# Block products of a triangular inverse with four blocks per matmul, zero-padded low-rank corrections, and another order of the parts

## The chip, the core and the metric

The kernel runs on one core of one Trainium2 chip. The core has five engines that run their own instruction queues and wait for each other by semaphores: TensorE (PE, matmuls into PSUM), VectorE (DVE), ScalarE (ACT), GpSimd (POOL) and SyncE (SP, which here issues nearly all DMAs). The metric is the device time of one execution in microseconds (us). The time before is 2999.29 us, the median of three runs (2991.41 to 3010.68).

## What is computed

Two layers of a hybrid network over 256 context tokens and 256 latent tokens, 1024 channels. Each layer has three token mixers (RWKV-7 in both directions, RG-LRU, neighbourhood attention), gates that merge them, and a gated MLP. The change touches the first mixer. Its core per head and direction is

```python
def step(S, inp):
    r_t, w_t, k_t, v_t, kk_t, a_t = inp
    sa = jnp.einsum('bhvk,bhk->bhv', S, -kk_t)
    S = (S * w_t[:, :, None, :] + sa[..., None] * (kk_t * a_t)[:, :, None, :]
         + v_t[..., None] * k_t[:, :, None, :])
    return S, jnp.einsum('bhvk,bhk->bhv', S, r_t)
```

with decay and a-gate made from low-rank products:

```python
w_log = -jax.nn.softplus(-(p['rwkv_w0'][d] + w_lo @ p['rwkv_w_up'][d])) - 0.5
a = jax.nn.sigmoid(p['rwkv_a0'][d] + a_lo @ p['rwkv_a_up'][d])
```

The kernel does the recurrence in chunks of 64 tokens. For each chunk it needs the inverse of a 64x64 unit triangular matrix: 2 heads, 2 directions and 8 chunks make 32 such matrices per pair of heads.

## The kernel before

All weights of a matmul come as one 512 KB tile from HBM. They are split into a high part (`wh`, ScalarE, L226) and a low part (`wl`, VectorE or GpSimd, L229), and `mm3` (L247 to L249) issues three matmuls of fp32r type per 128 rows. Activations have the same two parts (`hh`, `hl`). Tokens are 512 columns in layer 0. In layer 1 only 256 columns are wanted for most outputs. These `pj`, `pbr`, `wo`, `fg`, `fu`, `fo` matmuls are the bulk of the work.

A layer's mixers run over 8 pairs of heads. Per pair, the parts are letters in `CFG[l]['order']`: `1` and `2` make keys and prepare the next pair (`rw_key`, `rw_prep`), `g` the masked Gram products (`Gm`), `v` transposes (`bt`, and `BK` scaled in place), `i` the triangular solve of the 32x32 diagonal blocks on VectorE (`rw_inv`, L636 to L664), `I` the two products that fill the off-diagonal block (`rw_inv2`), `T` the sequence over 8 chunks (`rw_seq`: matmuls `r`, `sa`, `sp`, `yp`), `o`, `O`, `B` the output. The other letters are the other mixers: `X`, `Y`, `a`, `b`, `S` RG-LRU, `Q`, `A`, `P` attention, and `G`, `N` gate projections. `pri` gives a letter a priority. A scheduler turns order and priorities into one instruction list per engine, which the engine then follows strictly.

In `rw_inv2` VectorE transposes the solved blocks three times: L674 makes `T1` (tile `AT`), which the first product needs, L675 and L676 make parts of `TT` (tile `RT`). L676 is needed by the second product. The first product (L681, `Q<-AT,Gm`) is 32 matmuls of 32x32 by 32x32 in fp32, the second (L687, `Q<-RT,AT`) as many; the profile records each fp32 matmul as two, each with its own weight load. ScalarE copies each PSUM bank of 16 results back with one instruction (L682, L688). After them a DMA (L691) puts `KR` over the lower half of `Gm`, which `r` (L723) reads.

In `rw_prep` each direction multiplies the low-rank weights by activations that hold a high part in one half of the 128 rows and a low part in the other: `lh` (both halves the high weight) by all rows, then `ll` (low weights) by the 64 rows of the high part only:

```python
nc.tensor.matmul(pw, lhsT=lh[:, dc], rhs=self.wS, start=True, stop=False)
nc.tensor.matmul(pw, lhsT=ll[0:64, dc], rhs=self.wS[0:64], start=False, stop=True)
```

(L511, L512; L518, L519 for `pa`.) That is 2 such pairs for each of 2 directions, 8 pairs of heads and 2 layers.

## Time and profile before

| | before |
|---|---|
| median of three runs | 2999.29 us |
| profiled execution | 2999.59 us |
| span of its instructions | 2997.8 us |
| TensorE busy | 2834.2 us (95%) |
| VectorE busy | 1964.5 us (66%) |
| ScalarE busy | 1512.0 us (50%) |
| GpSimd busy | 595.7 us (20%) |
| mean granted TensorE clock | 0.957 |

The profile's page gives busy time per engine. Its views of waits, lines, stretches and the timeline say what an engine waited for and how long an instruction took. Matmuls overlap, so a matmul's own duration is longer than the distance between the starts of two. The distance is what it costs. Engine lines with one-line groups give busy time as the union of overlapping instructions.

### The profile page before, as it was taken

What the parts mean: (1) busy time and instruction counts of PE and PEld (TensorE: products, weight loads), DVE (VectorE), ACT (ScalarE), POOL (GpSimd) and SP (SyncE); (2) the same over time, 40 slices, a digit from 0 to 9 for tenths busy, and PEclk for the clock granted to TensorE, in tenths of its full rate; (3) what the DMA queues carried; (4) which work ended last, traced back from release to release, by engine and by line L of the source; (5) the groups of instructions that cost most, each with busy time, mean ns of one, the idle gap of its engine ahead of it and who ended that gap; (6) DMA issues with size and microseconds to landing.
All of it is one profiled execution on the core that took longest, in us unless ns stands there. A gap on an engine that the chain in (4) does not pass through costs nothing. (4 is left out here: it accounts for less than half of the span.)

```text
span 2997.8 us, 51813 instructions
## 1 busy us (share of the span) xinstructions
PE 2834.2 (95%) x20144; PEld 2263.7 (76%) x20144; DVE 1964.5 (66%) x3947; ACT 1512.0 (50%) x2917; POOL 595.7 (20%) x618
## 2 busy tenths in 40 slices
PE   7999999999999999989999998999999999989998
PEld 5777777777767677787778887777777777678898
DVE  6768777677776744475443268687778768755774
ACT  3565554556546542353333356655655665634453
POOL 2121120211202212200002211222221221212440
PEclk9999999999999999999999999999999998979899
DMA  6322122221222345755653452222222222236663
GB/s 226 94 70 74 56 89 64 72 68 53 87 69 68 106 158 182 255 184 182 218 175 92 121 172 83 65 78 77 67 72 82 64 64 78 87 104 211 219 195 115
DMA packets 159222, 344.30 MB, mean 115 GB/s; under 512 B 47488, under 2 KB 74368, under 8 KB 158976
## 3 DMA queue, kind: packets, MB, share of 16 engines
q1 hardware_dynamic: 152064, 334.69, 34.8%
q10 hardware_dynamic: 6912, 6.29, 0.7%
q8 instruction: 159, 2.61, 0.4%
q14 instruction: 87, 0.71, 0.1%
HBM read 301.08 MB, written 25.17 MB: 109 GB/s over the span
## 5 line engine op out<-in xcount | busy, mean ns | idle before, releaser
L226 ACT ACTIVATE wh<-wr 128x1024 fp32r<-128x1024 f32 (+1 forms) x402 | 420.1, 1046 | 537.4 <-PE pj L248 195.1
L247 PE MATMUL pj<-hh,wh 128*128 128x512 f32 (+1 forms) x1440 | 561.4, 391 | 22.6 <-DVE k L432 14.7
L229 DVE TENSOR_TENSOR wl<-wr,wh 128x1024 fp32r<-128x1024 f32 (+1 forms) x320 | 411.2, 1285 | 250.8 <-ACT wh L226 240.4
L249 PE MATMUL pj<-hh,wl 128*128 128x512 f32 (+1 forms) x1440 | 551.7, 384 | 8.2 <-POOL wl L229 4.1
L248 PE MATMUL pj<-hl,wh 128*128 128x512 f32 (+1 forms) x1440 | 551.3, 383 | 0.0
L247 PEld LDWEIGHTS pj<-hh,wh 128*128 128x128 f32 x1440 | 282.7, 196 | 83.0 <-issue 24.9
L249 PEld LDWEIGHTS pj<-hh,wl 128*128 128x128 f32 x1440 | 282.7, 197 | 61.8 <-issue 8.8
L229 POOL TENSOR_TENSOR wl<-wr,wh 128x1024 fp32r<-128x1024 f32 (+1 forms) x82 | 199.0, 2429 | 629.9 <-ACT wh L226 602.7
L248 PEld LDWEIGHTS pj<-hl,wh 128*128 128x128 f32 x1440 | 283.2, 197 | 47.1 <-issue 8.9
L741 POOL TENSOR_TENSOR sg<-SV,gC 64x128 f32<-64x128 f32 x192 | 114.3, 595 | 337.3 <-DVE SV L756 272.6
L660 DVE TENSOR_TENSOR itmp<-AT 128x126 f32<-128x126 f32 (+22 forms) x496 | 140.0, 282 | 11.2
L662 DVE TENSOR_TENSOR AT<-AT,itmp 128x126 f32<-128x126 f32 (+22 forms) x496 | 134.7, 272 | 10.8
L586 PEld LDWEIGHTS gram<-KR,BK 64*128 64x128 f32 x1024 | 120.5, 196 | 26.3 <-issue 13.9
L586 PE MATMUL gram<-KR,BK 64*128 64x128 f32 (+1 forms) x1024 | 136.6, 290 | 0.9 <-DVE Gm L589 0.4
L247 PE MATMUL fo<-fh,wh 128*128 128x256 f32 (+1 forms) x418 | 130.3, 312 | 0.0
L249 PE MATMUL fo<-fh,wl 128*128 128x256 f32 (+1 forms) x418 | 130.2, 311 | 0.0
L248 PE MATMUL fo<-fl,wh 128*128 128x256 f32 (+1 forms) x418 | 129.8, 310 | 0.0
L247 PE MATMUL fg<-hh,wh 128*128 128x256 f32 (+1 forms) x384 | 128.2, 336 | 1.1 <-ACT hh L403 1.1
L247 PE MATMUL fu<-hh,wh 128*128 128x256 f32 (+1 forms) x384 | 125.3, 327 | 2.7 <-DVE fgs L1356 2.0
L248 PE MATMUL fg<-hl,wh 128*128 128x256 f32 (+1 forms) x384 | 126.8, 331 | 0.0
L249 PE MATMUL fg<-hh,wl 128*128 128x256 f32 (+1 forms) x384 | 126.5, 330 | 0.0
L249 PE MATMUL fu<-hh,wl 128*128 128x256 f32 (+1 forms) x384 | 125.5, 328 | 1.0 <-DVE wl L229 1.0
(337 smaller groups left out, 6321.0 us busy)
## 6 DMA issues: line engine op xcount, KB each, us to landing
wr<-in_w_in SPq DMA_DIRECT2D x180, 512.0 KB, 3.3
aw<-in_ada_w SPq DMA_DIRECT2D x96, 512.0 KB, 4.6
wr<-in_ffn_w_in SPq DMA_DIRECT2D x96, 512.0 KB, 4.1
wr<-in_w_branch SPq DMA_DIRECT2D x48, 512.0 KB, 3.6
wr<-in_ffn_w_out SPq DMA_DIRECT2D x36, 512.0 KB, 3.6
wr<-in_w_out SPq DMA_DIRECT2D x24, 512.0 KB, 4.7
Gm<-KR SPq DMA_DIRECT2D x32, 256.0 KB, 4.3
wr<-in_ffn_w_out SPq DMA_DIRECT2D x18, 384.0 KB, 3.1
```

The lines of the kernel that those rows point to most:

```text
L226: nc.scalar.activation(hi, raw, AF.Copy)
L229: eng.tensor_tensor(lo, raw, hi.bitcast(F32), op=ALU.subtract)
L247: nc.tensor.matmul(o, lhsT=a, rhs=xh[k][:, n0:n1], start=(first and k == 0), stop=False)
L248: nc.tensor.matmul(o, lhsT=a, rhs=xl[k][:, n0:n1], start=False, stop=False)
L249: m = nc.tensor.matmul(o, lhsT=b, rhs=xh[k][:, n0:n1], start=False, stop=(last and k == kt - 1))
L586: nc.tensor.matmul(ps[:, i, 0:nx], lhsT=BK[hs, d, c, :], rhs=KR[hs, 0:nx, d, c, :], start=True, stop=True)
L660: eng.tensor_tensor(tmp, Ap[:, q + 1:32, q:q + 1].to_broadcast([P, nt, ns]), Tf[:, q:q + 1, 0:2 * ns:2].to_broadcast([P, nt, ns]), op=ALU. ...
L662: eng.tensor_tensor(Tf[:, q + 1:32, 0:2 * ns:2], Tf[:, q + 1:32, 0:2 * ns:2], tmp, op=ALU.subtract)
L741: nc.gpsimd.tensor_tensor(sg[64 * h:64 * h + 64], SV[0:64, i, :, h], gC[:, :, h, i:i + 1].to_broadcast([64, 2, 64]), op=ALU.mult)
```

## The change

1. The first product takes four blocks at once: the weights are four blocks side by side (32 rows, 128 columns), and the moving operand is four blocks of `T1` (128 columns). The result is 128x128, of which only the four 32x32 diagonal blocks are wanted. 8 matmuls replace 32. The second product is changed in the same way. ScalarE copies the diagonal blocks out with four instructions per bank in place of one.
2. With `f1` at 3 the blocks that the first product reads (`A10`) are first copied by VectorE into a corner of `BK` (32 rows, 1024 elements), and the `KR` to `Gm` DMA is issued in `rw_inv`, behind that copy, and no longer behind the products.
3. `ll` holds zeros where it was not read, and its matmuls use all 128 rows. VectorE makes two 64x256 pieces in place of one of 128x512, and GpSimd clears two 64x256 pieces.
4. Other orders, priorities and choices of engine in `CFG` for both layers; in layer 0 `oy` goes from 1 to 0, which makes the output transposes and gate product in one piece of 512 columns.

```diff
-  'order': '||g|ovOiXQIa||YbGSTA|12NPB|',
-  'oy': 1,
+  'order': '||g||o|vXQO|ia|I|Yb|GAT12SBNP||',
+  'oy': 0,
...
-  'order': 'gvGiIXabYSQA12TNPoOB',
+  'order': 'gGXviYaIb|SQA12TNPoOB',
...
-        self.split(lw[:, :512], lh, ll)
+
+        nc.scalar.activation(lh, lw[:, :512], AF.Copy)
+        for x in range(2):
+            rs, cs = slice(64 * x, 64 * x + 64), slice(256 * x, 256 * x + 256)
+            nc.vector.tensor_tensor(ll[rs, cs], lw[rs, cs], lh[rs, cs].bitcast(F32), op=ALU.subtract)
+            nc.gpsimd.memset(ll[rs, 256 - 256 * x:512 - 256 * x].bitcast(F32), 0.0)
...
-            nc.tensor.matmul(pw, lhsT=ll[0:64, dc], rhs=self.wS[0:64], start=False, stop=True)
+            nc.tensor.matmul(pw, lhsT=ll[:, dc], rhs=self.wS, start=False, stop=True)
...
-            nc.tensor.matmul(pa, lhsT=ll[64:128, dc], rhs=self.aS[64:128], start=False, stop=True)
+            nc.tensor.matmul(pa, lhsT=ll[:, dc], rhs=self.aS, start=False, stop=True)
...
-            ps = self.ps("q", "Q").rearrange("p (j t) -> p j t", t=32)
-            for i in range(16):
-                j = 16 * g + i
-                nc.tensor.matmul(ps[96:128, i, :], lhsT=A10[:, j], rhs=T1[0:32, j, :], start=True, stop=True)
-            nc.scalar.activation(T1[96:128, 16 * g:16 * g + 16, :], ps[96:128], AF.Copy, scale=-1.0)
+
+            ps = self.ps("q", "Q").rearrange("p (m a t) -> p m a t", a=4, t=32)
+            for m in range(4):
+                j = slice(16 * g + 4 * m, 16 * g + 4 * m + 4)
+                nc.tensor.matmul(ps[:, m].rearrange("p a t -> p (a t)"), lhsT=A10[:, j],
+                                 rhs=T1[0:32, j, :].rearrange("p a t -> p (a t)"), start=True, stop=True)
+            for a in range(4):
+                nc.scalar.activation(T1[96:128, 16 * g + a:16 * g + 16:4, :], ps[32 * a:32 * a + 32, :, a], AF.Copy, scale=-1.0)
```

The copied block is made by code that was there (`f1`):

```python
A10 = u["BK"][0:32, 0].rearrange("p c (x t) -> p (c x) t", t=32)
...
nc.vector.tensor_copy(A10, A0[0:32, :, 32:64])
for h in range(2):
    nc.sync.dma_start(G[0:64, 0, :, :, h], u["KR"][64 * h:64 * h + 64, 0])
```

TensorE's list at the inverse of the fourth pair of layer 1 (`pj` projections, `Q` the inverse products, `pa` low-rank products, `kst` the key norms, `r` the first step of the sequence). Before:

```order
L247 MATMUL pj_21745<-hh_15607,wh 128x512
L681 MATMUL Q<-AT,Gm 32x32 x32
L248 MATMUL pj_21745<-hl_15615,wh 128x512
L249 MATMUL pj_21745<-hh_15607,wl 128x512
L518 MATMUL pa<-aS,lh 128x512
L519 MATMUL pa<-aS,ll 128x512
L247 MATMUL pj_21745<-hh_15608,wh 128x512
L248 MATMUL pj_21745<-hl_15616,wh 128x512
L249 MATMUL pj_21745<-hh_15608,wl 128x512
L687 MATMUL Q_20598<-RT,AT 32x32 x16
L687 MATMUL Q_20616<-RT,AT 32x32 x16
L247 MATMUL pj_21745<-hh_15609,wh 128x512
```

and of the change:

```order
L249 MATMUL pj_20511<-hh_15231,wh 128x512
L689 MATMUL Q<-AT,BK 128x128 x8
L250 MATMUL pj_20511<-hl_15239,wh 128x512
L251 MATMUL pj_20511<-hh_15231,wl 128x512
L697 MATMUL Q_20289<-RT,AT 128x128 x4
L697 MATMUL Q_20298<-RT,AT 128x128 x4
L490 MATMUL kst<-cst,ta 128x2 x4
L250 MATMUL pj_20404<-hl_15234,wh 128x512
```

Two matmuls of 512 columns stand between the products where seven stood, and the next pair's keys and low-rank products come after the products, no longer ahead of them.

TensorE's list ahead of the inverse of the last pair of layer 1 (`pt`, `ao` attention; `pbr` the merge, `sa` the second step of the sequence). Before:

```order
L1063 MATMUL pt<-cst,pr 128x128 x4
L1074 MATMUL ao<-PT,vt 64x256
L1063 MATMUL pt<-cst,pr 128x128 x2
L1074 MATMUL ao<-PT,vt 64x256 x3
L1080 MATMUL ao<-PT,vt 64x64 x8
L681 MATMUL Q<-AT,Gm 32x32 x32
L687 MATMUL Q_25026<-RT,AT 32x32 x16
L687 MATMUL Q_25044<-RT,AT 32x32 x16
L723 MATMUL r_25310<-SV,Gm 128x128 x2
```

and of the change:

```order
L250 MATMUL pj_24947<-hl_15239,wh 128x256
L251 MATMUL pj_24947<-hh_15231,wl 128x256
L251 MATMUL pj_24704<-hh_15227,wl 128x512
L689 MATMUL Q<-AT,BK 128x128 x8
L249 MATMUL pj_24704<-hh_15228,wh 128x512
L250 MATMUL pj_24704<-hl_15236,wh 128x512
L697 MATMUL Q_24589<-RT,AT 128x128 x4
L251 MATMUL pj_24704<-hh_15228,wl 128x512
L249 MATMUL pj_24704<-hh_15229,wh 128x512
L250 MATMUL pj_24704<-hl_15237,wh 128x512
```

Projections now stand right up to the products. Between the last `bt` and the first `Q` of this pair the list of before has 9 matmuls of 512 columns and 46 of 256 among `pj` and `pbr`; the changed one has 37 and 72.

VectorE's list at the start of the solve of the fourth pair of layer 1 (`AT<-Gm` the transposes, `BK<-Gm` the new copy, `itmp` the first step of the solve, `xb` and `s` work of other mixers). Before:

```order
L636 STREAM_TRANSPOSE AT<-Gm 32x1024 x2
L984 TENSOR_TENSOR k<-sw 128x256
L649 COPY AT<-AT 64x1024
L660 TENSOR_TENSOR itmp<-AT 128x31
L662 TENSOR_TENSOR AT<-AT,itmp 128x31
```

and of the change:

```order
L643 STREAM_TRANSPOSE AT<-Gm 32x1024 x2
L231 TENSOR_TENSOR wl<-wr,wh 128x1024
L653 COPY BK<-Gm 32x1024
L656 COPY AT<-AT 64x1024
L842 SCALAR_TENSOR_TENSOR xb<-pj_20017,pv_13329,xb 128x2x254
L667 TENSOR_TENSOR itmp<-AT 128x31
```

The copy stands ahead of the solve and is one more instruction in that chain.

## Rows read from the trace of the kernel before

**Rows 1.** The page, part 1: busy us, share of span, instructions.
```profile
PE 2834.2 (95%) x20144; PEld 2263.7 (76%) x20144; DVE 1964.5 (66%) x3947; ACT 1512.0 (50%) x2917; POOL 595.7 (20%) x618
```

**Rows 2.** Cores: span, mean granted TensorE clock.
```profile
core 0: 2997.8 us, clock 0.957
```

**Rows 3.** TensorE's waits: us in total, times, longest us.
```profile
PE Q L681 <- DVE AT L674: 18.1, 12, 4.8
```

**Rows 4.** Timeline of TensorE at a low-rank pair: start us, us, instruction.
```profile
73.51 0.39 PE L247 MATMUL pj<-hh,wh 128*128 128x512 f32 x1
73.74 0.39 PE L248 MATMUL pj<-hl,wh 128*128 128x512 f32 x1
...
74.19 0.39 PE L511 MATMUL pw<-wS,lh 128*128 128x512 f32 x1
74.51 0.50 PE L512 MATMUL pw<-wS,ll 64*128 64x512 f32 x1
74.94 0.50 PE L247 MATMUL pj<-hh,wh 128*128 128x512 f32 x1
```

**Rows 5.** TensorE by line and form: count, busy us, mean ns, idle before.
```profile
L586 PE MATMUL gram<-KR,BK 64*128 64x128 f32 x768 | 110.7, 293 | 0.7 <-DVE Gm L589 0.4
...
L687 PE MATMUL Q<-RT,AT 32*32 32x32 f32 x1024 | 42.8, 205 | 0.8 <-DVE RT L676 0.8
...
L681 PE MATMUL Q<-AT,Gm 32*32 32x32 f32 x1024 | 39.8, 200 | 18.1 <-DVE AT L674 18.1
...
L519 PE MATMUL pa<-aS,ll 64*128 64x512 f32 x32 | 16.4, 514 | 0.0
L512 PE MATMUL pw<-wS,ll 64*128 64x512 f32 x32 | 16.3, 509 | 0.0
```

**Rows 6.** Timeline of TensorE: eight recorded fp32 128x128 passes in a row.
```profile
108.76 1.03 PE L621 MATMUL bt<-cst,BK 128*128 128x128 f32 x8
```

**Rows 7.** The page, part 5: weight loads of 64x128 in fp32.
```profile
L586 PEld LDWEIGHTS gram<-KR,BK 64*128 64x128 f32 x1024 | 120.5, 196 | 26.3 <-issue 13.9
```

**Rows 8.** Stretches around layer 1's last pair: us, busy by engine, PEclk, DMA, GB/s.
```profile
2480.00:2595.00 115.00, 107.44 (x760) 83.07 (x759) 83.53 (x184) 63.72 (x132) 22.95 (x31) 0.92 0.22 69
2595.00:2660.00 65.00, 50.14 (x379) 39.45 (x380) 45.35 (x119) 28.41 (x67) 5.06 (x5) 0.71 0.32 96
```

**Rows 9.** Stretches of 3.4 us: second products of one pair, then what follows.
```profile
524.40:527.80 3.40, 3.40 (x69) 2.70 (x68) 0.00 (x0) 0.88 (x2) 0.21 (x1) 1.00 0.47 113
527.80:531.20 3.40, 3.40 (x10) 2.63 (x9) 0.00 (x0) 0.60 (x2) 0.60 (x3) 0.50 0.02 5
```

**Rows 10.** The eleven half-clock stretches right behind inverse products: first, last, sum.
```profile
268.40:275.20 6.80, 6.80 (x56) 4.24 (x52) 4.37 (x3) 3.52 (x5) 0.00 (x0) 0.50 0.20 41
...
2528.00:2538.20 10.20, 10.20 (x81) 8.22 (x81) 4.79 (x8) 5.54 (x11) 1.99 (x4) 0.50 0.40 103
sum 78.20, PE 77.73 PEld 59.57 DVE 50.95 ACT 35.80 POOL 8.26; mean PE 7.07 PEld 5.42 DVE 4.63 ACT 3.25 POOL 0.75
```

**Rows 11.** ScalarE by line and form: copies out of PSUM.
```profile
L728 ACT ACTIVATE r<-r 64x128 f32<-64x128 f32 x256 | 69.2, 270 | 74.2 <-PE r L723 68.8 <-ACT wh L226 0.2
...
L682 ACT ACTIVATE AT<-Q 32x512 f32<-32x512 f32 x32 | 18.4, 588 | 40.4 <-PE Q L681 40.3
```

**Rows 12.** VectorE by line and form: transposes and copies of the solve.
```profile
L676 DVE STREAM_TRANSPOSE RT<-AT 32x1024 f32<-32x1024 f32 x16 | 31.4, 1961 | 0.2
L675 DVE STREAM_TRANSPOSE RT<-AT 32x1024 f32<-32x1024 f32 x16 | 30.7, 1916 | 0.5
...
L649 DVE COPY AT<-AT 64x1024 f32<-64x1024 f32 x16 | 11.0, 687 | 0.5
```

**Rows 13.** Timeline of TensorE at the products of layer 1's fourth pair.
```profile
2197.33 0.28 PE L247 MATMUL pj<-hh,wh 128*128 128x256 f32 x1
2197.45 0.28 PE L248 MATMUL pj<-hl,wh 128*128 128x256 f32 x1
...
2200.24 2.21 PE L681 MATMUL Q<-AT,Gm 32*32 32x32 f32 x64 [1.45 <-DVE AT L674]
```

More of the change, by code (lines that the diff above doesn't have):

```diff
@@ L50 @@
 C2O = {n: (256 * i, 256) for i, (n, _) in enumerate(_C2)}
-CFG = [{'f1': 0,
-  'ff': [40000, 12000],
-  'fg': 0,
-  'fi': 20000,
-  'hp': 10000,
+CFG = [{'f1': 3,
+  'ff': [40000, 0],
+  'fg': 4,
+  'fi': 10000,
+  'hp': 20000,
   'lo': {'1': [0],
-         'G': [0, 1],
+         'G': [0, 1, 1, 1],
          'N': [1, 0],
@@ L78 @@
   'no': 5,
-  'order': '||g|ovOiXQIa||YbGSTA|12NPB|',
-  'oy': 1,
+  'order': 'g||o|vXQO|ia|I|Yb|GAT12SBNP||',
+  'oy': 0,
   'pe': [0, 0, 0, 0, 0, 0, 0],
@@ L83 @@
           '2': 5000,
-          'B': 400,
+          'B': 20000,
           'O': 5000,
+          'P': 400,
           'S': 10000,
           'T': 5000,
-          'a': 5000,
+          'a': 200,
+          'b': 0,
           'g': 1200,
@@ L106 @@
   'fi': 0,
-  'hp': 20000,
+  'hp': 10000,
   'lo': {'1': [0],
-         'G': [0, 1],
-         'N': [0],
-         'Q': [0],
+         'G': [0],
+         'N': [0, 1],
+         'Q': [0, 0, 0, 0, 0, 1],
          'X': [1],
          'Y': [0],
-         'fi': [0, 1, 1, 0, 1],
+         'fi': [1, 1, 1, 0],
          'fo': [0],
-         'fp': [0, 0, 1, 0],
-         'm0': [0],
-         'm1': [0, 1, 0, 0],
-         'st': [0],
+         'fp': [1, 0, 0, 0, 0],
+         'm0': [0, 0, 1, 1, 0, 1],
+         'm1': [0],
+         'st': [1, 0],
          'wo': [0]},
@@ L149 @@
   'rw': 1,
-  'sp': [0.04, 0.43, 0.47, 0.47, 0.72],
+  'sp': [0.0, 0.4, 0.54, 0.55, 0.56],
   'sq': 0,
-  'st': -1,
+  'st': 0,
   'sw': 0,
-  'wo': [25000, 15000],
+  'wo': [600, 15000],
   'yo': 1}]
@@ L677, in rw_inv2 @@
         for g in range(2):
[L678 to L688 removed]
+            ps = self.ps("q", "Q").rearrange("p (m a t) -> p m a t", a=4, t=32)
[5 more added lines that the diff above has]
+                nc.scalar.activation(T1[96:128, 16 * g + a:16 * g + 16:4, :], ps[32 * a:32 * a + 32, :, a], AF.Copy, scale=-1.0)
+        for g in range(2):
+            ps = self.ps("q", "Q2").rearrange("p (m a t) -> p m a t", a=4, t=32)
+            for m in range(4):
+                j = slice(16 * g + 4 * m, 16 * g + 4 * m + 4)
+                nc.tensor.matmul(ps[:, m], lhsT=T1[96:128, j, :].rearrange("p a t -> p (a t)"), rhs=TT[32:64, j, 32:64],
+                                 start=True, stop=True)
+            for a in range(4):
+                nc.scalar.activation(TT[0:32, 16 * g + a:16 * g + 16:4, 32:64], ps[32 * a:32 * a + 32, :, a], AF.Copy)
         if not self.cfg['f1']:
```

39 lines of the change are left out of this document (17 added, 22 removed).

## The prediction

> **What bounds the kernel now.** I read the busy times first, then TensorE's waits, then the lines and the timeline at the places that the diff names. TensorE is busy for 2834.2 of 2997.8 us [rows 1, 2], so 163.6 us are idle. Nothing else is near: VectorE stands at 66%, ScalarE at 50%. A us of work taken from TensorE is therefore worth nearly a us, as long as no new wait takes its place. The mean clock is 0.957, and the clock is either whole or half, so (1 - 0.957) / 0.5 = 8.6% of the span, some 258 us, ran at half clock. That is a second place where time can come from. The largest single wait of TensorE is at the line that the diff rewrites: 18.1 us in 12 times until the transpose of the solved blocks (L674) is ready [rows 3].
>
> The sum is made against the profiled execution's 2999.6 us, which is its span and 1.8 us around it. The median of the three runs is 2999.3 us, so they can be read as one.
>
> **Low-rank pairs: -19 us.** Two projections of 512 columns start 0.23 us apart (73.51, 73.74). The high product starts at 74.19, its 64-row partner 0.32 us later and the next projection 0.43 us after that [rows 4]. The pair takes 0.75 us where two plain matmuls take 0.46, and all three shapes stream the same 512 columns. With 128 rows in both, the 0.29 us should go. There are 32 + 32 such pairs [rows 5]: 64 x 0.29 = 18.6 us. Bounds: 12 us, where a neighbour of another shape keeps part of it, and 20. VectorE gets two pieces in place of one and GpSimd two small fills per pair of heads; at 20% GpSimd hides them, and the consumer comes many matmuls later.
>
> **Inverse products: -20 us.** They hold TensorE for 42.8 + 39.8 = 82.6 us [rows 5]. Afterwards there are 16 pairs of heads x 16 matmuls x 2 recorded passes = 512 passes of 128 columns. No row shows 32 rows by 128 columns. The nearest in width is a run of eight fp32 passes of 128x128 in 1.03 us [rows 6]. The first is 0.28 us long, so the others are (1.03 - 0.28) / 7 = 0.107 us apart, and 512 of them are 54.8 us. The nearest in use of few rows is the Gram product, 110.7 / 768 = 0.144 us each, gaps at the ends of short groups included [rows 5], which gives 73.8 us. I take 62, nearer the dense row since the groups are eight and sixteen passes long: 82.6 - 62 = 20 us saved, between 9 and 28.
>
> Here a rule speaks against the change. The Trainium skill (TensorE: Matmul & The Clock Gate, Part 3, The mechanism) says that a weight load overlaps matmuls in flight only when its row group differs. All eight matmuls of one product use the same 32 rows, so by that rule each pass would wait for its own load. The trace does not agree: the eight passes of the dense row use the same 128 rows, each has its load, and they still follow each other by 0.107 us. It is one of the rivals below.
>
> **Last pair of layer 1: -13 us.** This stretch is unlike its neighbours: 50.1 us busy in 65, at a clock of 0.71, against 107.4 in 115 at 0.92 just before [rows 8]. TensorE has run out of projections there and waits for the solve. At the neighbour's idle share (7.6 of 115) the 65 us would hold 4.3 us of idle time and not 14.9, so 10.6 us are to be had. The new order puts 28 more matmuls of 512 columns and 26 more of 256 between the last transposes and the products. At 0.23 us [rows 4] and 0.12 us (2197.33 to 2197.45) [rows 13] that is 6.4 + 3.1 = 9.5 us of cover, and the whole idle excess less 1. The clock adds something: 50.1 us at 0.71 is 35.6 us of full-clock work, which at 0.92 takes 38.7. I take 10 for the idle part and 3 of these 11. Bounds: 0, if the work is only missing elsewhere, and 22.
>
> **Clock behind the products: -18 us.** In one stretch of 3.4 us TensorE was busy all the time, two thirds of it with 32x32 products, at full clock; in the next 3.4 us it had only projections and the granted clock was 0.50 [rows 9]. So the small products can bring the clock down with no idle time at all. Eleven half-clock stretches, 78.2 us together, start right behind such products [rows 10], which is 39 us of lost full-clock time. The change makes them four times as wide and fewer. In the other cases there is also an idle wait before the product, which stays. I take a little under half, 18 us. Bounds: 0 and 39.
>
> **New waits between the products and the sequence: +14 us.** ScalarE copies each bank with four instructions. A copy of 128 columns takes 0.27 us (nearest row: 64 rows by 128), one of 512 columns 0.588 [rows 11]: 4 x 0.27 - 0.59 = 0.49 us more for each of 64 banks, 31 us of ScalarE work. At 50% it has room, but each bank is on the chain product, copy, product, copy, `sa`. Before, seven matmuls stood between the two products of layer 1's middle pairs; now there are two or three, and `r` and `sa` follow closely. After L674, L675 and L676 take 1.92 + 1.96 = 3.9 us more [rows 12]. Where the first product starts the moment L674 ends, its 16 passes (0.28 + 15 x 0.107 = 1.9 us) and two matmuls (0.46) leave 1.5 us of waiting before the second, which the 2.21 us of the old product and the seven matmuls hid (the second line lost 0.8 us in all [rows 5]). Half of eight pairs x 1.5 is 6 us; `sa` behind the longer copies, 0.5 us in 16 pairs, is 8. Bounds: 3 and 40 us (16 x 1.5 and 16 x 1.0).
>
> The Trainium skill (TensorEngine Tiling, PSUM Bottleneck) warns that a faster product does not speed up what empties PSUM, which may then be the limit. By that the copies would set the pace of this short chain in every pair; the row of 0.27 us says that four cost about twice one.
>
> **Longer solve chain: +6 us.** The copy into `BK` adds one VectorE instruction ahead of the solve. The nearest row is a copy of as many elements, 0.69 us; the upper bound is a transpose of the same 32x1024, 1.96 us [rows 12]. I take 0.7. Twelve pairs wait for this chain today [rows 3], by 1.5 us each as in layer 1's fourth pair [rows 13], so 12 x 0.7 = 8 us at most; longer cover in some pairs takes 2 of them. Bounds: 0 and 31 (16 x 1.96). The `KR` DMA moves ahead of the products. I cost it at nothing: it then waits for a copy at the start of the solve, and no longer for products at its end, so it lands earlier. If SP is held there, weight tiles queue behind it; three raw buffers cover that. I also put the one-piece output of layer 0 at nothing: the same columns are streamed.
>
> **The sum:** -19 - 20 - 13 - 18 + 14 + 6 = -50, so 2999.6 - 50 = **2950 us**. The rest of the reordering, on engines with room, I cannot price from rows; it widens the range on both sides.
>
> **The rivals.** A measurement of this kernel can tell about 1%, 30 us, from no change, so the borders are 2969 and 3029.
>
> *More than forecast.* The new matmuls run at the dense rate (-28), the clock recovers behind all products (-39), the last pair gains 22 and the waits stay at their lower bounds: -20 - 28 - 22 - 39 + 3 = -106, or 2894 us. For it speaks the stretch with no idle time whose clock still fell; against it the 18.1 us of waiting that no edit removes. Chance 0.16, with all between it and 2925.
>
> *The gain is given back.* The chain of copies is exposed in every pair (+40) and, since each wait is idle time at the same place, the clock does not recover: -19 - 20 - 13 + 40 + 6 = -6, or 2994 us. For it speaks how closely the new lists put the second product and `sa` behind the first; against it that ScalarE is free half of the time. Chance 0.20.
>
> *Weight loads do not overlap.* Each of 512 passes then also pays its load, 120.5 / 1024 = 0.118 us of the load engine's time [rows 7], or 60 us: 2950 + 60 = 3010 us. This is what the rule named above would give. The dense row speaks against it. Chance 0.04.
>
> *Slower.* In layer 1 the copied block lies in `BK`, so the next pair's preparation can write there only after the first product, and the new list puts that pair's keys and low-rank products behind it. If the preparation is then late for the next Gram product, TensorE idles there in every pair of layer 1. It decides from 80 us on, that is 10 us in each of 8 pairs: 2950 + 80 = 3030. Nothing in the trace of before shows such a wait (keys came ahead of the products); for it speaks only the order. Chance 0.08.
>
> *The forecast*, 2925 to 2969: chance 0.52.
>
> **How the numbers follow.** Faster by over 1%: 0.52 + 0.16 = 0.68. Within 1%: 0.20 + 0.04 = 0.24. Slower: 0.08. The range reaches from 2900, near the case of more, to 2990, near the case of the gain given back; about a tenth is left out on each side.
>
> **What would show it.** Low-rank: the low product starts 0.23 us behind the high one and the next matmul 0.23 us behind it. Products: the two lines together busy for 55 to 74 us. Last pair: that stretch busy for over 90% and its clock over 0.85. Clock: the mean at 0.96 or more and fewer half-clock stretches behind the products. New waits: rows of TensorE's waits for `Q` on L676's successor and on ScalarE's copies, and `sa` on ScalarE, 10 to 20 us together. Solve: `Q` on the transpose near 24 us. I am wrong if TensorE's idle time grows by more than 30 us over 163.6, or if the products' lines are not shorter.

## The result and the profile after

The changed kernel takes 3025.19 us (median of eight runs, 3014.33 to 3034.99) and the kernel before, run beside it, 3002.73 us (eight runs, 2987.45 to 3012.85). The ratio is 1.0069, 95% interval 1.0046 to 1.0093: it is slower by 0.7%, where 2950 us were forecast. The profiled execution took 3028.23 us. Its page, part 1 (busy us, share, instructions), and its core (span, mean granted TensorE clock), against [rows 1, 2]:

```profile
PE 2848.1 (94%) x18592; PEld 2291.8 (76%) x18592; DVE 1959.6 (65%) x3968; ACT 1539.1 (51%) x3101; POOL 617.2 (20%) x645
```

```profile
core 0: 3026.4 us, clock 0.944
```

The clock is whole or half, so the time at half clock is (1 - 0.944) / 0.5 x 3026.4 = 339 us, against 258 before. These 81 us more cost 40 us. TensorE is busy for 13.9 us longer; without the 40 us of clock its work has fallen by 26 us. Its idle time is 178.3 us against 163.6, 15 us more. The sum -26 + 40 + 15 = 29 us is the 28.6 us by which the span grew. So the work went down, by 26 of the 39 us that were forecast for the products and the low-rank pairs, and the clock took it back.

TensorE's waits (us in total, times, longest). For the first product [rows 3] has 18.1 us; before, the second product waited for 0.8 us [rows 5] and `r` behind `SV` for 0.9.

```profile
PE Q L689 <- DVE AT L681: 20.0, 13, 2.3
...
PE r L735 <- DVE SV L768: 4.7, 10, 0.8
...
PE Q L697 <- DVE RT L683: 4.6, 6, 1.3
...
PE gram L593 <- POOL ll L476: 0.4, 1, 0.4
...
PE sa L757 <- ACT r L740: 0.2, 1, 0.2
```

TensorE by line and form (count, busy us, mean ns, idle before): the products and the low parts of the low-rank pairs, against [rows 5].

```profile
L697 PE MATMUL Q<-RT,AT 32*128 32x128 f32 x256 | 52.8, 382 | 4.7 <-DVE RT L683 4.6
L689 PE MATMUL Q<-AT,BK 32*128 32x128 f32 x256 | 39.7, 314 | 20.0 <-DVE AT L681 20.0
```

```profile
L526 PE MATMUL pa<-aS,ll 128*128 128x512 f32 x32 | 13.3, 416 | 0.0
L519 PE MATMUL pw<-wS,ll 128*128 128x512 f32 x32 | 13.1, 408 | 0.0
```

The low parts are shorter, as forecast. The products are not: 92.5 us against 82.6, although only a quarter of the instructions is left. The timeline of one pair of layer 1 shows why (start us, us, instruction, idle before):

```profile
2311.09 2.14 PE L689 MATMUL Q<-AT,BK 32*128 32x128 f32 x16 [2.05 <-DVE AT L681]
2313.16 0.80 PE L250 MATMUL pj<-hl,wh 128*128 128x512 f32 x1
2313.76 0.63 PE L251 MATMUL pj<-hh,wl 128*128 128x512 f32 x1
2315.06 3.75 PE L697 MATMUL Q<-RT,AT 32*128 32x128 f32 x16 [0.68 <-DVE RT L683]
2318.74 1.22 PE L735 MATMUL r<-SV,Gm 128*128 128x128 f32 x4
```

The first product runs mostly at full clock, 2.07 us from start to next start. Then the clock halves: two projections are 0.60 us apart instead of 0.23, and the second product takes 3.68 us for the same 16 passes. Fourteen half-clock stretches stand at or right behind the products, 181.1 us together, where [rows 10] has eleven with 78.2 us. Counted alike in both traces, from the first pass of the first product to 15 us behind the second, half clock lasts 180 us in the 16 pairs and 100 before. These 80 us are the whole of what was added. The first of the fourteen stretches, the longest and the sum (us, busy by engine, PEclk, DMA, GB/s):

```profile
148.90:155.70 6.80, 6.80 (x29) 5.27 (x29) 0.58 (x2) 1.02 (x5) 0.79 (x2) 0.50 0.00 0
...
2097.90:2118.40 20.50, 19.84 (x82) 17.15 (x82) 12.35 (x22) 8.54 (x24) 7.84 (x10) 0.50 0.10 33
...
sum 181.10, PE 177.10 PEld 143.30 DVE 94.71 ACT 97.11 POOL 36.30; mean PE 12.65 PEld 10.24 DVE 6.77 ACT 6.94 POOL 2.59
```

The stretch ahead of layer 1's last products, which [rows 8] shows with 50.14 us busy of 65 at a clock of 0.71, is now filled:

```profile
2600.80:2665.80 65.00, 60.11 (x320) 44.99 (x319) 48.43 (x119) 37.68 (x78) 6.59 (x6) 0.85 0.28 81
```

### The profile page after: what moved, and what is told of

Same layout as the page of the kernel before. It is cut to its first block, busy times and chain, and to the rows that moved or that the text cites. A ratio compares the mean times of both kernels' runs of the same rounds, so it can differ in the third digit from the quotient of the medians.

```text
span 3026.4 us, 49006 instructions
## 1 busy us (share of the span) xinstructions
PE 2848.1 (94%) x18592; PEld 2291.8 (76%) x18592; DVE 1959.6 (65%) x3968; ACT 1539.1 (51%) x3101; POOL 617.2 (20%) x645
## 4 chain that ended last, share of the span: by engine, by line
PE 51%; DVE 11%; issue 6%; DMA 4%; ACT 3%; POOL 2%; SPq 0%; POOLq 0%; DVEq 0%; ACTq 0%
PE pj L249 4%; PE pj L250 4%; PE pj L251 4%; PE gram L593 3%; DMA aw<-in_ada_w 2%; PE fu L251 2%; PE fu L249 2%; PE fu L250 2%; PE pbr L249 2%; PE r L735 2%; PE pbr L251 2%; PE sa L757 2%; PE fg L249 2%; PE pbr L250 2%; PE fg L250 2%
## 5 line engine op out<-in xcount | busy, mean ns | idle before, releaser
L249 PE MATMUL pj<-hh,wh 128*128 128x512 f32 (+1 forms) x1440 | 572.1, 399 | 24.1 <-DVE xb L844 11.1
L251 PE MATMUL pj<-hh,wl 128*128 128x512 f32 (+1 forms) x1440 | 559.1, 389 | 6.8 <-DVE wl L231 4.6
L250 PE MATMUL pj<-hl,wh 128*128 128x512 f32 (+1 forms) x1440 | 563.8, 392 | 0.1
L231 POOL TENSOR_TENSOR wl<-wr,wh 128x1024 fp32r<-128x1024 f32 (+1 forms) x85 | 205.5, 2421 | 546.3 <-ACT wh L228 525.8
L753 POOL TENSOR_TENSOR sg<-SV,gC 64x128 f32<-64x128 f32 x192 | 108.2, 563 | 292.8 <-DVE SV L768 233.6
L768 DVE TENSOR_TENSOR SV<-sp,sg 64x128 f32<-64x128 f32 x192 | 55.0, 286 | 126.2 <-PE sp L763 121.3
```

The source lines that it names most:

```text
L231: eng.tensor_tensor(lo, raw, hi.bitcast(F32), op=ALU.subtract)
L249: nc.tensor.matmul(o, lhsT=a, rhs=xh[k][:, n0:n1], start=(first and k == 0), stop=False)
L250: nc.tensor.matmul(o, lhsT=a, rhs=xl[k][:, n0:n1], start=False, stop=False)
L251: m = nc.tensor.matmul(o, lhsT=b, rhs=xh[k][:, n0:n1], start=False, stop=(last and k == kt - 1))
L753: nc.gpsimd.tensor_tensor(sg[64 * h:64 * h + 64], SV[0:64, i, :, h], gC[:, :, h, i:i + 1].to_broadcast([64, 2, 64]), op=ALU.mult)
L768: nc.vector.tensor_tensor(SV[0:64, i + 1, :, h], pp[hs, :, h], sg[hs], op=ALU.add)
```

## The experiments

Each run has a span and a mean clock. I split the span into a **full-clock length** (span x clock: what it would take with the clock always whole, waits included) and a **clock loss** (span x (1 - clock)). This is an account: what waits for another engine does not shrink with TensorE's clock, so a clock that recovers can show as a longer full-clock length. Both are means over all runs of a kernel, with their standard error. For the kernel before they are 2867.0 +- 0.7 and 132.8 +- 1.7 us in the 25 runs of one chip, and between 2867 and 2870, and 125 and 132, on the others. The median of before differs by up to 8 us between chips, so a difference to before, here and below, is always taken to the runs of before on the same chip. For the changed kernel they are 2861.0 +- 1.5 and 161.3 +- 3.4: shorter by 6, and 28 us more lost by the clock.

| run | us | ratio to before, 95% interval | full-clock length | clock loss |
|---|---|---|---|---|
| lowrank_alone | 2990.37 | 0.9955 (0.9939 to 0.9971) | 2861.2 +- 1.2 | 126.3 +- 2.2 |
| order_alone | 3017.07 | 1.0044 (1.0028 to 1.0061) | 2886.1 +- 1.0 | 128.3 +- 2.2 |
| products_alone | 3063.30 | 1.0203 (1.0182 to 1.0225) | 2886.2 +- 2.4 | 175.8 +- 2.9 |
| products_lowrank | 3056.45 | 1.0176 (1.0153 to 1.0198) | 2879.2 +- 1.3 | 174.7 +- 2.5 |
| copy_alone | 3041.59 | 1.0154 (1.0128 to 1.0181) | 2879.7 +- 3.4 | 161.2 +- 5.5 |
| four_copies | 3032.89 | 1.0121 (1.0096 to 1.0147) | 2875.7 +- 2.2 | 155.3 +- 4.3 |
| rows128 | 3062.81 | 1.0223 (1.0200 to 1.0246) | 2914.4 +- 2.5 | 146.9 +- 2.5 |
| first_only | 3079.41 | 1.0283 (1.0254 to 1.0312) | 2889.3 +- 1.2 | 189.3 +- 3.1 |
| fixed_copy | 3010.37 | 1.0035 (1.0007 to 1.0063) | 2873.8 +- 1.1 | 135.5 +- 4.5 |
| fixed_products | 3025.95 | 1.0081 (1.0056 to 1.0107) | 2870.2 +- 1.5 | 155.1 +- 4.5 |
| fixed_lowrank | 2969.28 | 0.9892 (0.9861 to 0.9923) | 2860.0 +- 1.7 | 108.4 +- 5.6 |
| late_order_old_products | 3011.77 | 1.0036 (1.0015 to 1.0058) | 2853.9 +- 1.0 | 157.5 +- 2.3 |
| fixed_rows128 | 2984.56 | 0.9946 (0.9927 to 0.9966) | 2884.8 +- 0.6 | 99.0 +- 1.8 |
| after_filled | 3011.11 | 1.0041 (1.0019 to 1.0063) | 2872.9 +- 1.0 | 137.6 +- 2.3 |
| after_filled2 | 3005.07 | 1.0007 (0.9979 to 1.0034) | 2896.2 +- 1.1 | 106.0 +- 4.4 |
| lowrank_filled | 2978.96 | 0.9926 (0.9902 to 0.9951) | 2868.7 +- 1.1 | 109.1 +- 3.7 |
| after_rows128 | 3011.21 | 1.0053 (1.0028 to 1.0078) | 2877.2 +- 0.6 | 129.9 +- 2.3 |
| lowrank_rows128 | 2986.36 | 0.9968 (0.9945 to 0.9991) | 2874.9 +- 1.5 | 109.9 +- 3.9 |

### One part at a time, lists made anew

The theory at this point (theory A in the expectations) was that the new order costs what the change loses; the rival (theory B) was that the wide products themselves bring the clock down.

**lowrank_alone**: only the three edits of the low-rank parts.

```diff
-            nc.tensor.matmul(pw, lhsT=ll[0:64, dc], rhs=self.wS[0:64], start=False, stop=True)
+            nc.tensor.matmul(pw, lhsT=ll[:, dc], rhs=self.wS, start=False, stop=True)
...
```

> The kernel before with the padded low-rank part alone (old products, old order). Both theories expect the same: the partner of each high product starts 0.23 us behind it and the next matmul 0.23 us later, 64 pairs x 0.29 us = 12 to 19 us less, so a ratio of 0.994 to 0.996. If it is not faster, the row that priced it was misread.

Measured: 12.6 us faster than before, at the low end.

**order_alone**: only the new `CFG` of both layers (with `f1` at 3, so the copied block too). The order of layer 0 in it, and in the changed kernel, is `g||o|vXQO|ia|I|Yb|GAT12SBNP||`; the `||` that the listing of the change shows ahead of `g` is not in the kernel.

> The kernel before with the new CFG alone, which is the new order with the copied block (old 32x32 products, old low-rank part). Theory A: most of the loss is here, 1.008 to 1.015, with half-clock time of 310 us or more. Theory B: within 0.3% of before, half-clock time near 258 us.

Measured: 14 us slower, and by the full-clock length (+17), not by the clock. That is between the two theories.

**products_alone**: the four-block products and `f1` at 3, in the old `CFG`.

> The kernel before with the four-block products and the copied block alone (old order, old low-rank part). Theory A (the new order is what costs: it sets both products, r and sa close together, and the clock falls there): in the old order the products gain the little they gain at full clock, 16 x 2 x 0.16 = 5 us, less the copy, so a ratio of 0.996 to 1.001 and half-clock time near the 258 us of before. Theory B (a product of 32 rows by 128 columns lowers the clock by itself, whatever stands around it): slower by 20 us or more, 1.006 and up, and half-clock time of 310 us or more.

Measured: 60 us slower, 44 of them by the clock. This is the opposite of what theory A wants, and what theory B wants, but with the copied block and new lists in it.

**products_lowrank**: the same with the padded low-rank parts.

> Four-block products, copied block and padded low-rank part in the old order. Theory A: the sum of the two gains, 15 to 25 us faster, 0.991 to 0.995. Theory B: the low-rank gain against the loss of the products, 0.999 to 1.004.

Measured: 53 us slower, which neither theory wants; the low-rank parts take off 7 here, not 13. The parts one by one give -12.6 + 14 + 60 = +62 us and the whole change +22. Two things stand in the way of such a sum: the copied block is in both of the last two, and the scheduler makes every engine's list anew for each variant.

### Inside the products

**copy_alone**: `f1` at 3 and nothing else.

```diff
-CFG = [{'f1': 0,
+CFG = [{'f1': 3,
...
```

> The kernel before with nothing but the copy of the block into BK ahead of the solve (and with it the KR transfers that move to that place); the old products, order and low-rank parts. The four-block products in the old order, which carry this copy with them, took 3063 us against 3003. If the copy and the moved transfers are the cause (theory copy: a solve chain one VectorE instruction longer, 12 waits longer by 0.7 to 2 us each, and the clock falls in them), this run takes 3030 us or more. If the cause lies in the products or in what empties their banks, it takes 3003 us, within 10, and the half-clock time stays near 258 us.

Measured: 47 us slower. A copy of 0.68 us per pair cannot be that; either it or the lists had to be shown apart (fixed_copy, below).

**four_copies**: as copy_alone, with each bank of the old products emptied in quarters.

```diff
-            nc.scalar.activation(T1[96:128, 16 * g:16 * g + 16, :], ps[96:128], AF.Copy, scale=-1.0)
+            for a in range(4):
+                nc.scalar.activation(T1[96:128, 16 * g + a:16 * g + 16:4, :], ps[96:128, a:16:4], AF.Copy, scale=-1.0)
...
```

> As copy_alone, with the old 64 small passes in each product, but each bank is emptied by four ScalarE instructions of a quarter each, as the four-block products need it. Theory chain (product, four copies, product, four copies, sa is longer, TensorE idles in it and the clock falls): 3040 us or more, idle time above 180 us, half-clock time above 330 us. Theory form (the 32x128 passes themselves keep the clock down): within 12 us of copy_alone, half-clock time within 20 us of it.

Measured: 9 us below copy_alone, with 175 us of idle time and 327 at half clock. That speaks against theory chain, but TensorE's list in the trace is not that of copy_alone, so the copies are not the only difference. fixed_products, below, has the four copies in held lists.

**first_only**: the new first product, the old second one, in the old `CFG`.

> Only the first of the two products takes four blocks at once (with the copied block and its four copies of a bank); the second is the old one with one copy of a bank; old order. Theory chain: about half of the extra 60 us, 3025 to 3040 us, since half of the extra copies is gone. Theory form: the second product, which in the changed kernel runs at half clock for most pairs, takes its 2.1 us at 32x32 as before, and the clock comes back behind it as before: 3003 to 3020 us. If the first product alone brings the clock down: 3050 us or more.

Measured: 85 us slower, more than both products together (60). This is the third of the expected cases; the first product is under suspicion, but with new lists again.

**rows128**: products_alone, and the first product reads 128 rows; GpSimd writes zeros under the block in each pair.

```diff
-                nc.tensor.matmul(ps[:, m].rearrange("p a t -> p (a t)"), lhsT=A10[:, j],
-                                 rhs=T1[0:32, j, :].rearrange("p a t -> p (a t)"), start=True, stop=True)
+                nc.tensor.matmul(ps[:, m].rearrange("p a t -> p (a t)"), lhsT=u["Z"][:, j],
+                                 rhs=T1[:, j, :].rearrange("p a t -> p (a t)"), start=True, stop=True)
```

> The four-block products in the old order (3063 us), with the first product read over all 128 rows instead of 32: the block lies over 96 rows of zeros that GpSimd writes, and T1 has finite numbers there. Passes, columns and copies are the same. Theory form, in the variant that few rows in use let the clock fall: the half-clock stretches that follow the first product shrink from 130 us to 90 or less and the time falls to 3045 us or less. Theory chain, or form without regard to rows: 3063 us, within 10, half-clock time near 368 us.

Measured: 68 us slower than before, where products_alone was 60, and made up differently. Against before on its own chip the clock takes 22 us (44 in products_alone), and the full-clock length is 45 us longer (17). Inconclusive, since the zeros lie on the path and the lists differ.

### With every engine's list held

From here on the scheduler was not left to choose. The list of each engine was read from the kernel before (or from the changed one), and every instruction got an edge to its predecessor there that fixes the order of issue and waits for nothing. New instructions stand where the old ones stood, and the `KR` transfer stays in its place. In the traces TensorE's list is then the one it was made from, apart from the products. The kernel before with held lists and no edit was not run, so what the holding itself costs or gives is not shown.

```diff
+            for a, b in zip(o, o[1:]):
+                tc.add_manual_dep(b, a.name, _mybir.DependencyInfo(_mybir.DependencyClass.NoSync, _mybir.DependencyReason.DATA), reason="pinned")
```

In the lists of before the copied block gets a tile of its own. The solve starts ahead of the last transposes of `BK` there (105 and 110 us in the first pair), so a copy into `BK` ahead of the solve has no place in them.

**fixed_copy**:

```diff
-            A10 = u["BK"][0:32, 0].rearrange("p c (x t) -> p (c x) t", t=32)
+            A10 = R.tile([32, 32, 32], F32, tag="A10", name="A10")
```

> The kernel before with each engine's list held exactly as it was, and one instruction more on VectorE per pair: the copy of the block ahead of the solve. It goes to a tile of its own and not to BK, so nothing else has to move. copy_alone (copy into BK, lists made anew by the scheduler) took 47 us more than before. Theory list (the cost comes from the lists that the scheduler makes once the block lies in BK): 3003 to 3012 us, since the copy is some 0.7 us on a chain for which 12 pairs wait. Theory copy (the instruction itself, by a longer solve chain): 3035 us or more. Half-clock time near 258 us by the first, above 300 us by the second.

Measured: 9 us slower, 7.1 +- 1.4 of them full-clock length. That is the size that its place on the chain says. But the wait that a longer chain should lengthen did not change; it is 18.0 us where [rows 3] has 18.1, so where the 7 us lie is not shown:

```profile
PE Q L681 <- DVE AT L674: 18.0, 12, 4.8
```

Of the 47 us of copy_alone some 38 come with the lists that go with the block in `BK`.

**fixed_products**:

> As fixed_copy, and both products take four blocks at once with four copies of each bank, every new instruction at the place of the old ones and all other instructions in the order of before. Theory list: the products give 32 x 0.16 = 5 us at full clock and lose a little on the longer copies, so within 12 us of fixed_copy, and half-clock time within 30 us of it. Theory form (the wide products themselves keep the clock down or expose the chain of copies): 25 us or more above fixed_copy, half-clock time 40 us or more above it. The forecast on record would want some 38 us below before.

Measured: 15.6 us above fixed_copy. The full-clock length is 3.6 us shorter and the clock loses 19.6 +- 6.4 us more. The busy times of the two profiled executions say the same of the work (fixed_copy, then fixed_products; by their clock records 296 and 332 us at half clock, 35 more):

```profile
PE 2849.8 (94%) x20144; PEld 2277.0 (75%) x20144; DVE 1972.3 (65%) x3963; ACT 1513.4 (50%) x2917; POOL 594.1 (20%) x618
```

```profile
PE 2862.1 (94%) x18608; PEld 2282.0 (75%) x18608; DVE 1974.1 (65%) x3963; ACT 1545.4 (51%) x3109; POOL 592.2 (20%) x618
```

Busy time is up by 12.3 us, of which 17.6 are clock: the wide products save 5 us of work. Of these the full-clock length shows 3.6 +- 1.9, so the longer chain of copies on ScalarE costs little here. The time lies between the bounds of both theories; the work speaks for theory list, the clock for theory form.

**fixed_lowrank**:

> The kernel before with each engine's list as it was, and only the low-rank parts padded to 128 rows. lowrank_alone, whose lists the scheduler made anew, gained 13 us. If that is the work alone, this gains 12 to 19 us as well (2984 to 2991 us); if its lists had a share in it by luck, this differs by more than 8 us from it.

Measured: 32 us faster, about twice what was expected. The full-clock length is only 6.7 us shorter; 23.4 +- 6.1 us come from the clock. With busy time 40.9 us shorter and the clock at 0.964 (210 us at half clock by its record, 48 less than before), 24 us are clock and 17 us are work, near the 18.6 of the prediction. Idle time grew by 7 us (171.0 against 163.6). Its page, and a pair in its timeline, where [rows 4] has 0.32 and 0.43 us between starts and this 0.22 and 0.23:

```profile
PE 2793.3 (94%) x20144; PEld 2248.5 (76%) x20144; DVE 1972.8 (67%) x3963; ACT 1511.5 (51%) x2917; POOL 602.5 (20%) x650
```

```profile
73.80 0.39 PE L516 MATMUL pw<-wS,lh 128*128 128x512 f32 x1
74.02 0.39 PE L517 MATMUL pw<-wS,ll 128*128 128x512 f32 x1
74.25 0.39 PE L247 MATMUL pj<-hh,wh 128*128 128x512 f32 x1
```

This is the fastest version measured: 0.9892 of before.

**late_order_old_products**: the lists of the changed kernel, with the old products in them.

> The changed kernel with each engine's list held exactly as it is there (copy into BK, padded low-rank parts, new order), but with the old products: 32 small matmuls and one copy of a bank, at the places of the new ones. Theory list: the order of the changed kernel is what costs, so this stays at 3015 to 3030 us. Theory form: without the wide products the changed kernel falls to 3000 us or less, and its half-clock time from 338 to 280 us or less.

Measured: 3011.77 us, between the two expectations. By the medians the wide products cost 13 us in the new order; by the split it is 7.1 us of full-clock length and 4 +- 4 of clock. So with the old products these lists lose 157.5 us by the clock, 26 more than before in spite of the padded low-rank parts: most of the 28 us of the changed kernel is here already. The waits for VectorE are here too:

```profile
PE Q L694 <- DVE RT L683: 4.7, 8, 1.1
PE r L730 <- DVE SV L763: 4.7, 10, 0.8
```

And the order, with the block in `BK`, can be told from the rest: against before, less the 6.7 us of fixed_lowrank and plus the 7.1 of fixed_copy, it makes the full-clock length 2853.9 - 2866.7 + 6.7 - 7.1 = 13 us shorter. The clock loss grows by 157.5 - 131.8 + 23.4 - 3.7 = 45 us in the same sum, if losses add (the last run says that they do not). This holds for these lists: order_alone, the same `CFG` with other lists, had 17 us more of full-clock length and 3 less of clock loss.

### What brings the clock down

Open then was the clock. One theory (rows) was that products that use a quarter of the rows let it fall, the other (wait) that the idle time ahead of the product does.

**fixed_rows128**: fixed_products with the block in a tile whose other rows are set to zero once per layer, and 128 rows in the first product.

```diff
+        self.A10z = Q.tile([P, 32, 32], F32, tag="A10z", name="A10z")
+        nc.gpsimd.memset(self.A10z, 0.0)
...
-                nc.tensor.matmul(ps[:, m].rearrange("p a t -> p (a t)"), lhsT=A10[:, j],
-                                 rhs=T1[0:32, j, :].rearrange("p a t -> p (a t)"), start=True, stop=True)
+                nc.tensor.matmul(ps[:, m].rearrange("p a t -> p (a t)"), lhsT=u["Z"][:, j],
+                                 rhs=T1[:, j, :].rearrange("p a t -> p (a t)"), start=True, stop=True)
```

> fixed_products (3026 us; full-clock length 2870, clock loss 155 us), with the first product read over all 128 rows: the copied block lies in rows 0 to 31 of a tile whose other rows were set to zero once per layer, and T1 is finite there. No instruction is added inside the pairs. Theory rows (a product that uses a quarter of the rows lets the clock fall): the clock loss falls to 140 us or less and the time to 3011 us or less. Theory wait (what matters is the idle time ahead of the product): 3026 us, within 9, clock loss 145 to 165 us.

Measured: 41 us faster than fixed_products; the clock loss falls from 155.1 to 99.0 us. The same pair of layer 1 in the timelines, first fixed_products, then fixed_rows128. The list is the same, and so is the wait of 1.45 us:

```profile
2218.15 2.05 PE L682 MATMUL Q<-AT,A 32*128 32x128 f32 x16 [1.45 <-DVE AT L674]
2220.12 0.50 PE L248 MATMUL pj<-hl,wh 128*128 128x512 f32 x1
...
2222.63 0.63 PE L248 MATMUL pj<-hl,wh 128*128 128x512 f32 x1
2223.06 0.63 PE L249 MATMUL pj<-hh,wl 128*128 128x512 f32 x1
2223.61 3.78 PE L690 MATMUL Q<-RT,AT 32*128 32x128 f32 x16
2227.32 0.80 PE L247 MATMUL pj<-hh,wh 128*128 128x512 f32 x1
```

```profile
2199.33 2.05 PE L685 MATMUL Q<-AT,A10z 128*128 128x128 f32 x16 [1.45 <-DVE AT L677]
2201.14 0.48 PE L248 MATMUL pj<-hl,wh 128*128 128x512 f32 x1
...
2202.77 0.39 PE L248 MATMUL pj<-hl,wh 128*128 128x512 f32 x1
2203.00 0.40 PE L249 MATMUL pj<-hh,wl 128*128 128x512 f32 x1
2203.44 2.08 PE L693 MATMUL Q<-RT,AT 32*128 32x128 f32 x16
2205.45 0.79 PE L247 MATMUL pj<-hh,wh 128*128 128x512 f32 x1
```

Behind a first product of 32 rows the clock is halved (starts 0.43 us apart, the second product 3.71 us to the next start). Behind one of 128 rows it stays whole (0.23 us, 2.01 us) and falls only behind the second product, which still uses 32 rows. Over all 16 pairs, from the first product to 15 us behind the second, half clock lasts 131 us in the trace of fixed_products and 34 in that of fixed_rows128. The wait did not change, so it is the rows over which the product is issued. In three quarters of them the weights are zero. A product of 128 rows also has the shape of the matmuls around it; whether the clock answers to the number of rows or to the change of shape was not told apart.

**after_filled**: the changed kernel, with six throwaway matmuls of 128 rows and 512 columns ahead of each first product.

```diff
+            for _ in range(6 * (g == 0)):
+                nc.tensor.matmul(p0, lhsT=self.wS[:, 0:128], rhs=self.wS, start=True, stop=True)
```

> The changed kernel (3025 us; full-clock length 2861, clock loss 161 us) with its lists held, and six throwaway matmuls of 128x512 (1.4 us) ahead of the first product of each pair, written to the PSUM bank that the product overwrites; 13 of 16 pairs wait there for 1.5 us on average. Theory wait: they lie in the wait, so the full-clock length grows by 8 us at most, and the clock loss falls by 25 us or more: 3008 us or less. Theory rows, or that the clock falls by what comes after the first product: the loss stays within 12 us of 161, and the time is 3025 to 3040 us.

Measured: 14 us faster than the changed kernel, with 24 us less lost by the clock and 12 us more of full-clock length. It misses each of the three bounds of theory wait narrowly (8 us, 25 us, 3008) and is far from the other. In this order full-row work ahead of the product does give clock back.

**after_filled2**: four more ahead of each second product.

> As after_filled, with four more throwaway matmuls (0.9 us) ahead of the second product of each pair, where TensorE waits for 4.6 us in 6 pairs and for the copies of ScalarE. If the clock falls between the two products, since only two or three matmuls stand there in the new order, this loses at least 20 us less by the clock than after_filled and is faster than it; if not, it is 5 to 15 us slower than after_filled, by the 16 x 0.9 us of added work less what lies in waits.

Measured: 3005 us; the clock loss is 32 us less than in after_filled, and the full-clock length is 23 us longer. In the new order the clock is kept up by full-row work between the two products, which that order has little of: two projections in the timeline of after, seven matmuls in the old one. The added work eats most of it; 6 us between medians of ten runs that spread over 44 is not clear of noise.

**lowrank_filled**: the six matmuls in fixed_lowrank.

> fixed_lowrank (2969 us; full-clock length 2860, clock loss 108 us) with the six throwaway matmuls ahead of the first product of each pair. Theory wait: the half-clock stretches behind the first product (41 us in 7) shrink, the loss falls to 95 us or less and the time to 2955 to 2968 us. If the wait is not what brings the clock down: 2970 to 2985 us, by the matmuls of the pairs that don't wait.

Measured: 10 us slower, the clock loss unchanged (109.1 against 108.4), although the wait ahead of the first product shrank from 20.1 to 5.6 us. In the old order filling that wait gives no clock back.

**after_rows128**: the changed kernel with its lists, and the first product over 128 rows as in fixed_rows128.

> The changed kernel with its lists held (3025 us; full-clock length 2861, clock loss 161 us), the block copied into the tile whose other rows are zero, and the first product read over all 128 rows; nothing else is changed, and no instruction is added inside the pairs. Theory rows: the clock loss falls by 40 to 60 us and the full-clock length grows by up to 15, as in fixed_rows128: 2970 to 3000 us. If in this order something else brings the clock down (the wait between the products, the order): loss 145 us or more, 3015 us or more.

Measured: the clock loss falls by 31 us, to 130 (before has 127 on this chip). So one product over 128 rows takes away what the change had added, which the old products of 32 rows had lost in these lists too: the loss needs both this order and the 32 rows. But the time falls only by 14 between the medians, and from 1.0069 to 1.0053 of before, since the full-clock length grows by 16. That lies between the two expectations. The waits show half of that: TensorE now comes too early for the transposes.

```profile
PE Q L692 <- DVE AT L684: 19.1, 13, 2.3
...
PE Q L700 <- DVE RT L686: 12.6, 10, 1.6
```

The second product waits for 12.6 us instead of 4.6. VectorE's transposes do not follow TensorE's clock (1.94 us in the mean in the changed kernel, 1.96 here); time at half clock between the products had hidden them.

**lowrank_rows128**: fixed_rows128 with the padded low-rank parts.

> fixed_rows128 (2985 us) with the padded low-rank parts as well, in the lists of before: all that gained, without the new order. If the gains add (16 us of fixed_rows128, 32 of fixed_lowrank): 2953 us. If both only take the same clock loss away, which cannot fall twice: 2965 to 2972 us, no better than fixed_lowrank.

Measured: 2986 us, worse than both expectations, no better than fixed_rows128 and 17 us behind fixed_lowrank. The clock loss is 110 us: against before on the same chips the two parts give back 34 and 23 us alone and 17 together. So the gains do not add; why they give less than either alone is not shown. The full-clock length is 7 us above before, as with the copy alone.

## Why the prediction was wrong

The step that failed is **"Clock behind the products: -18 us"**. It had the right row [rows 9]: small products bring the clock down with no idle time. It then took "four times as wide and fewer" as a cure, and put the new order, which leaves two matmuls between the products where seven stood, into the waits alone. Width is no cure: 64 passes of 32 columns and 16 of 128 both stream 2048 columns, both over 32 rows, in 2.14 and 1.97 us at full clock. With held lists the wide products lost 20 +- 6 us more by the clock than the old ones in the old order, and 4 +- 4 more in the new one; nothing came back in either. The order costs clock: with the old products in the new lists 26 of the 28 us of extra loss are there. What counts beside it is the rows: reading the first product over 128 takes 31 us of the loss away. Measured in the term's place: 28 us more clock loss in the mean of the runs, 40 us in the profiled execution, so the term was wrong in sign.

**Inverse products, -20.** Mis-sized: about -5 us of work. The new price was right: 16 passes take 1.97 us at full clock (2218.15 to 2220.12), 32 times that is 63 us, and 62 were taken. But it was subtracted from 82.6 us of busy time that held half-clock passes. A full-clock product of before, the one of [rows 13], takes 2.14 us to the next start (2200.24 to 2202.38), 32 of them 68.5. Two prices at one clock would have given -5:

```profile
2202.38 0.50 PE L248 MATMUL pj<-hl,wh 128*128 128x512 f32 x1
```

By busy time 32 such products are 32 x 2.21 = 70.7 us. The other 12 of the 82.6 were half clock, which the clock's term claimed in part as well.

**Low-rank pairs, -19.** Right in the work (17 us, starts 0.22 and 0.23 us apart). Not foreseen: in the lists of before idle time takes back 7, and the clock gives 23.

**Last pair of layer 1, -13.** Right for the stretch: it is 92% busy at 0.85, with 4.9 us idle where 14.9 stood. The order as a whole shortens the full-clock length by 13 us in held lists; that the two figures agree is luck, since it did much else. The same order loses by the clock, by 26 us measured directly and 45 by the sum above; which of its moves does that was not tried one by one.

**New waits, +14.** Idle time grew by 15 us in all, so the size is near, but by luck. The second product waits for VectorE, for which 6 us were forecast (4.6 against 0.8); `sa` on ScalarE, 8 us of the term, waits for 0.2. Not named was `r` behind `SV`, 4.7 us against 0.9. Both waits for VectorE are as long with the old products in the same lists (4.7 and 4.7), so they come from the order. The four copies cost little: each takes 0.267 us as forecast, and with the wide products idle time is 4 us more in the new lists (178.3 against 174.0). The full-clock length is 7.1 us more there; where the rest comes from is not shown.

**Solve chain, +6.** The price is right (the copy takes 0.678 us), and so is the size: fixed_copy's full-clock length is 7.1 us longer. The way is not shown: the wait for the transpose, for which about 24 us were forecast, stayed at 18.0 there and is 20.0 in the changed kernel.

```profile
L653 DVE COPY BK<-Gm 32x1024 f32<-32x1024 f32 x16 | 10.9, 678 | 0.5 <-PE bt L628 0.2
```

```profile
L692 ACT ACTIVATE AT<-Q 32x128 f32<-32x128 f32 x128 | 34.2, 267 | 34.9 <-PE Q L689 32.7
```

**The rivals.** *Gain given back*, in whose band 3025 lies, named the right balance, work gained and lost again, but by 40 us of exposed copies and a clock that does not recover; it was 15 us of idle time and a clock that got worse. *Slower* named the wrong mechanism: the Gram product waits for 0.4 us in all. *Weight loads do not overlap* is out: 16 passes in the same 32 rows follow each other by 1.97 / 16 = 0.123 us; a load of 0.118 us in front of each pass of 0.107 would make 0.225. Of the two signs named for being wrong, idle time grew by 15 and not by 30, and the products' lines did get longer.

**What stays open.** The lists that the scheduler makes anew can move the time by more than an edit: the same copy costs 9 us in held lists and 47 in new ones, where it goes into `BK`. Why those lists lose 36 us by the clock is not settled. Nor is it shown why the wide products lose 20 us more by the clock in the old lists, with as few rows as the old ones. The second product was not tried over 128 rows. Nor is it shown why the padded low-rank parts gain 23 us by the clock in the old lists and 5 in lists made anew; the old lists have one such pair between the products, but that it keeps the clock up there was not tried.

## What to carry to other kernels

Compare prices at one clock: take a line's busy time apart into its full-clock price and its half-clock share before subtracting. A matmul that uses a quarter of the rows can take as long as a full one by itself (1.97 us against 1.81 here) and still leave half clock behind it. Where the other rows can be zeros, reading all 128 cost the product nothing here and gave back 56 and 31 us of clock, while the full-clock length grew by 15 and 16. Work of 128 rows between two such products also gave clock back (32 us), but cost 23 of them. With a scheduler behind the kernel, hold the lists to measure one edit, since otherwise the new lists are measured with it.

## What the runs showed of the hardware

- In one pair of layer 1, 16 passes of 128 rows by 128 columns took 1.81 us to the next start (2199.33 to 2201.14) and 16 of 32 rows 1.97 us, with the same 128 columns. Fewer rows saved nothing, and behind the 32-row passes the granted clock was 1.2 GHz and not 2.4. In the 16 pairs together, half clock lasted 34 us at and behind the products with 128 rows in the first, and 131 with 32.
- Clock that comes back is not all time: with 56 us less of clock loss fixed_rows128 had 15 us more of full-clock length, and after_rows128 16 us more for 31. In after_rows128 8 of them are a longer wait for VectorE.
- Clock losses do not add: 108 us with the padded low-rank parts, 99 with the padded product, 110 with both, against 127 to 133 without on the same chips.
- The same program with the same list differs from run to run by its clock: fixed_copy took 2991 us at a mean clock of 0.961 and 3024 at 0.950.
